# Gated delta rule with four operands to a norm, the first shift on TensorE, and modulation units placed by a weight

## The chip, the cores and the metric

One core of a Trainium2 chip. The metric is the device time of one execution of the whole program, in microseconds. All operands are fp32; the large projections are carried out as three matmuls each, on a weight and an activation that are split into a high and a low part.

## The reference

Two transformer blocks stand one behind the other, T = 256 tokens, D = 1024. Each norm is modulated by rows of `silu(c) @ w + b`, six rows of 1024 per layer in the first block, nine in the second. The first layer of the first block is attention, the second the gated delta rule:

```python
mod = (silu(c) @ ada_w[layer] + ada_b[layer])
shift_m, scale_m, gate_m, shift_f, scale_f, gate_f = split(mod, 6)
h = rmsnorm(x, norm_mix_g) * (1.0 + scale_m) + shift_m        # then attention or:
qkv = silu(conv(h @ w_in))                                    # 8 heads of 128
q = q * rsqrt(sum(q * q) + EPS) * 128 ** -0.5
k = k * rsqrt(sum(k * k) + EPS)
o = chunk_gated_delta_rule(q, k, v, g, beta)                  # decay, triangular inverse
o = rmsnorm(o, norm_g) * silu(z);  x = x + gate_m * (o @ w_out)
h = rmsnorm(x, norm_ffn_g) * (1.0 + scale_f) + shift_f;  x = x + gate_f * swiglu(h)
```

The second block has, in each of two layers, a half-step FFN, a mixing layer and another half-step FFN, on two streams of 256 tokens (the last FFN on one).

## The kernel before

Activations lie transposed, features on the partitions, in eight tiles of 128 x 256. A projection of one weight unit (1024 x 128) is 24 matmuls: eight tiles times three products (`mm3`, lines 405 to 407).

All weights come from memory in one list, `PLAN`, of 783 units of up to 512 KB. `mat` units feed matmuls. `mod` units are 128 columns of a modulation matrix, transposed; VectorE multiplies such a unit by the broadcast `silu(c)` and sums along the row (`mod_unit`, line 491), twice in the second block, whose two streams have a condition each. There are 240. `pump` (line 361) issues the loads on SP's queue up to twelve units ahead, into nine raw buffers, and splits up to three matmul units ahead: ScalarE casts (line 378), VectorE subtracts (line 379). `get` (line 384) hands out the next matmul unit and first works off the modulation units before it. `_evenly` (line 48) sets the modulation units at equal distances among a part's matmul units, after some at its front and before some at its end.

The instructions of each engine are put in one order when the program is built: by their place in the program and by when a planner thinks that their operands are there. Each engine then keeps to its order and waits where it must. A unit of modulation can so stand well ahead of the place that `PLAN` gives it.

The start (`build`, line 1412): the condition is loaded 128 times over, the positions too, the rope tables are made on VectorE, the squares of x are added up by GpSimd (line 551) and summed by a matmul with ones; eight `mod` units for the scale and eight for the shift go through VectorE, then `scale` (line 853), `shift` (lines 860, 861), and the first projection.

The delta-rule layer (`gdn`, line 1103): projections, convolutions and silu of heads 0 to 3; the norms (`gdn_norm`); decay and products of each head (`gdn_mats`); the inverse of two pairs of heads (`gdn_inverse`, line 1026), woven with the projections of heads 4 to 7; reading (`gdn_read`), and the same for heads 4 to 7, woven with the projections of z. A norm squares on ScalarE, sums over the partitions by a 128-column matmul of ones (line 559), which leaves the sum in all partitions, and runs `rsq` (line 515) for each operand of 256 columns: logarithm, exponential and a scaled copy on ScalarE, three instructions on VectorE (lines 522 to 524); then VectorE multiplies. There are 24 such operands: q and k of eight heads, and eight outputs.

The FFNs (`ffn`, line 623) run in three parts: gate and up units, then eight output units of the part. With two streams a matmul has 512 columns.

## Time and profile before

| what | value |
|---|---|
| runs, median of 3 | 2502.35 us (2498.07 to 2504.37) |
| profiled execution | 2497.55 us |
| its span, first to last instruction | 2495.7 us |
| mean granted TensorE clock | 0.994 |
| TensorE busy | 2391.3 us (96%) |
| VectorE busy | 1786.3 us (72%) |
| ScalarE busy | 1073.5 us (43%) |
| moved from memory | 408.66 MB, 164 GB/s over the span |

A page gives shares of the whole span; a stretch view gives the same for part of it. PE is TensorE, DVE VectorE, ACT ScalarE, POOL GpSimd, SP the engine that issues most loads. A busy TensorE has a matmul in flight, whose end is modelled; starts are measured.

### The profile page before, as it was taken

The page shows a single profiled execution, that of the slowest core. Times are in us where ns is not written, and L with a number is a line of the kernel's source. Part 1 is how long each engine was busy: PE and PEld are TensorE (multiplying, and loading weights), DVE is VectorE, ACT ScalarE, POOL GpSimd, SP SyncE. Part 2 cuts the span into 40 slices and gives each one's busy share as a digit, 9 for nine tenths or more (in the row PEclk, how much of TensorE's full clock was granted, in tenths as well). Part 3 has the DMA queues.
Part 4 walks back from the last instruction along what each step waited for, and adds up shares of the span by engine and source line. Part 5 has one row for each costly group of instructions (what it writes and reads, how often), then busy time and mean ns, then how long its engine had stood idle before and what let it go on. Part 6 is the DMA issues. An engine that isn't in the chain of part 4 may idle for free.

```text
span 2495.7 us, 38415 instructions
## 1 busy us (share of the span) xinstructions
PE 2391.3 (96%) x14963; PEld 2130.3 (85%) x14963; DVE 1786.3 (72%) x3087; ACT 1073.5 (43%) x1879; POOL 169.9 (7%) x172
## 2 busy tenths in 40 slices
PE   3999998899999999999999999999999999999998
PEld 2889998898999888888886888888988878988998
DVE  8987779886897997763657597663687663675765
ACT  3554455566644622223537432223432223456444
POOL 1000000414100100000010100000100000111000
PEclk9999999999999999999999999999999999999999
DMA  9766676432786475542220265452365452242652
GB/s 332 271 223 227 225 236 225 153 102 90 263 265 209 161 236 191 173 162 99 79 79 33 85 219 178 153 182 87 109 201 180 160 175 95 83 131 77 205 183 70
DMA packets 118406, 412.21 MB, mean 165 GB/s; under 512 B 13136, under 2 KB 16464, under 8 KB 118224
## 3 DMA queue, kind: packets, MB, share of 16 engines
q1 hardware_dynamic: 113904, 402.28, 47.7%
q10 hardware_dynamic: 4320, 7.47, 0.9%
q8 instruction: 118, 1.93, 0.3%
q14 instruction: 64, 0.52, 0.1%
HBM read 408.66 MB, written 1.05 MB: 164 GB/s over the span
## 4 chain that ended last, share of the span: by engine, by line
PE 76%; DVE 9%; DMA 8%; issue 3%; ACT 2%; POOL 1%; DVEq 0%; ACTq 0%; SPq 0%; POOLq 0%
PE pmm L405 21%; PE pmm L406 21%; PE pmm L407 21%; DMA r<-w 7%; DVE l L379 2%; DVE r L491 2%; DVE junk L491 2%; PE pax L1026 2%; PE pmm L1348 1%; PE pax L407 1%; PE pax L406 1%; PE pax L405 1%; PE pnm L1387 1%; PE pax L1358 1%; ACT h L378 1%
## 5 line engine op out<-in xcount | busy, mean ns | idle before, releaser
L378 ACT CAST h<-r 128x1024 fp32r<-128x1024 f32 (+2 forms) x543 | 549.6, 1017 | 992.4 <-PE pmm L406 907.3
L379 DVE TENSOR_TENSOR l<-r,h 128x1024 fp32r<-128x1024 f32 (+2 forms) x543 | 645.0, 1192 | 195.6 <-ACT h L378 188.2
L405 PE MATMUL pmm<-h,h 128*128 128x512 f32 (+1 forms) x1916 | 668.3, 350 | 31.3 <-ACT h L860 23.1
L406 PE MATMUL pmm<-h,h 128*128 128x512 f32 (+1 forms) x1916 | 664.7, 347 | 1.8 <-DVE h L593 1.6
L407 PE MATMUL pmm<-h,l 128*128 128x512 f32 (+1 forms) x1916 | 662.3, 346 | 0.0
L405 PEld LDWEIGHTS pmm<-h,h 128*128 128x128 f32 x1916 | 364.1, 190 | 78.1 <-ACT h L860 23.8
L406 PEld LDWEIGHTS pmm<-h,h 128*128 128x128 f32 x1916 | 364.2, 190 | 48.5 <-DVE h L593 3.7
L407 PEld LDWEIGHTS pmm<-h,l 128*128 128x128 f32 x1916 | 364.2, 190 | 44.7 <-issue 0.2
L405 PE MATMUL pmm<-hid,h 128*128 128x256 f32 (+1 forms) x1053 | 349.8, 332 | 6.2 <-DVE s L633 2.7
L406 PE MATMUL pmm<-hid,h 128*128 128x256 f32 (+1 forms) x1053 | 348.3, 331 | 1.5 <-DVE hid L444 1.5
L407 PE MATMUL pmm<-hid,l 128*128 128x256 f32 (+1 forms) x1053 | 348.0, 331 | 0.7 <-DVE l L379 0.7
L405 PE MATMUL pmm<-hb,h 128*128 128x258 f32 x1008 | 286.4, 284 | 5.7 <-ACT hb L581 4.2
L407 PE MATMUL pmm<-hb,l 128*128 128x258 f32 x1008 | 284.9, 283 | 0.0
L406 PE MATMUL pmm<-hb,h 128*128 128x258 f32 x1008 | 284.9, 283 | 0.0
L491 DVE SCALAR_TENSOR_TENSOR junk<-r,cnd 128x1024 f32<-128x1024 f32 x144 | 175.9, 1221 | 125.9 <-DMA r<-w 122.6
L405 PEld LDWEIGHTS pmm<-hid,h 128*128 128x128 f32 x1053 | 200.4, 190 | 26.3 <-ACT hid L443 3.9
L406 PEld LDWEIGHTS pmm<-hid,h 128*128 128x128 f32 x1053 | 200.4, 190 | 20.9 <-DVE hid L444 2.4
L407 PEld LDWEIGHTS pmm<-hid,l 128*128 128x128 f32 x1053 | 200.5, 190 | 19.3 <-DVE l L379 1.1
L405 PEld LDWEIGHTS pmm<-hb,h 128*128 128x128 f32 x1008 | 190.8, 189 | 7.3 <-ACT hb L581 5.0
L406 PEld LDWEIGHTS pmm<-hb,h 128*128 128x128 f32 x1008 | 191.7, 190 | 0.4 <-DVE hb L582 0.2
L407 PEld LDWEIGHTS pmm<-hb,l 128*128 128x128 f32 x1008 | 191.7, 190 | 0.1
L491 DVE SCALAR_TENSOR_TENSOR r<-r,cnd 128x1024 f32<-128x1024 f32 x144 | 176.1, 1223 | 5.5 <-ACT cnd L464 2.4
(332 smaller groups left out, 2867.8 us busy)
## 6 DMA issues: line engine op xcount, KB each, us to landing
r<-w SPq DMA_DIRECT2D x665, 512.0 KB, 4.2
r<-w SPq DMA_DIRECT2D x96, 448.0 KB, 3.4
r<-w SPq DMA_DIRECT2D x16, 256.0 KB, 2.5
cnd<-cond ACTq DMA_DIRECT2D x8, 512.0 KB, 4.6
r<-w SPq DMA_DIRECT2D x6, 384.0 KB, 3.2
const<-const SPq DMA_DIRECT2D x2, 960.0 KB, 6.3
x<-xT ACTq DMA_DIRECT2D x8, 128.0 KB, 5.7
x<-ctxT ACTq DMA_DIRECT2D x8, 128.0 KB, 2.6
```

Source lines behind the costliest of these rows:

```text
L378: nc.scalar.copy(h[:, :n], r[:, :n])
L379: nc.vector.tensor_tensor(lo[:, :n], r[:, :n], h[:, :n].bitcast(F32), op=OP.subtract)
L405: nc.tensor.matmul(out, wh, ah, start=start, stop=False)
L406: nc.tensor.matmul(out, wh, al, start=False, stop=False)
L407: nc.tensor.matmul(out, wl, ah, start=False, stop=stop)
L491: nc.vector.scalar_tensor_tensor(o, r, 1.0, self.conds[ns - 1 + s], op0=OP.mult, op1=OP.mult, accum_out=t[:, 8 * s + m:8 * s + m + 1])
L1026: nc.tensor.matmul(p[:, s], a[:, s], b[:, s], start=True, stop=True)
L1348: self.nc.tensor.matmul(s, q, k, start=True, stop=True)
L1358: self.nc.tensor.transpose(p[:, 128 * b:128 * b + 128], P[:, 128 * b:128 * b + 128], self.ident)
L1387: nc.tensor.matmul(o[64 * a:64 * a + 64, 128 * qt:128 * qt + 128], V[2 * s + b][:, h], pts[a][:, 128 * b:128 * b + 128], start=b == 0, sto ...
```

## The change

Four things change.

- The placement: `_place` spreads the modulation units by a weight (`room`) of each matmul unit instead of by count. In FFNs an output unit weighs 1.0, a gate or up unit 0.5, within a window. In the delta-rule layer the units stand behind those of heads 4 to 7 (weight 2) and of z (1); the eight of its scale move into the first FFN. `get` issues the loads and splits of all units passed before it works off their modulation.
- The start: the shift's eight units are taken untransposed as `rows` units; `mod_rows` multiplies them on TensorE by `silu(c)` in one of 32 columns, four quarters of 256 into four strips of 32 partitions, adds up over eight units, copies, transposes twice and adds the bias. The condition and positions are loaded as rows and spread by a matmul with ones; ones is set by GpSimd instead of loaded; the squares of x are added up by TensorE; half of the x loads go on SP's queue; the gain is finished column by column; the norm precedes the rope tables; the first query unit is taken ahead of the last two row units.
- The norms of the delta rule: four operands are summed into four strips of 32 partitions (`norms`), go through one `rsq`, and are spread again by a matmul with a selecting matrix (`spread`) into PSUM, from which VectorE multiplies 512 columns at once. The scale of q moves into `gdn_mats`.
- `rsq` has one `y` buffer instead of two.

```diff
-def _evenly(units, mods, a, b):
+def _place(units, mods, room):
+    room = [room(i, u[1]) for i, u in enumerate(units)]
+    out, k, c, total = [], 0, 0.0, sum(room)
+    for u, w in zip(units, room):
         out.append(u)
-        while k < len(mods) and i >= a + k * n // len(mods):
+        c += w
+        while k < len(mods) and c * len(mods) >= (k + 1 - 1e-6) * total:
             out.append(mods[k])
             k += 1
+    assert k == len(mods)
+def _ffn_room(a, b):
+    return lambda i, key: (1.0 if key[1] == "o" else 0.5) if a <= i < b else 0.0
...
-    u += _evenly(q, A(0, 2, 3, 4), 4, 0)
+    rows = [("rows", ("ada_w", 0, 0, kt), [("ada_w", 0, kt * 128, 0, 1024)]) for kt in range(KT)]
+    u = A(0, 1) + rows[:6] + q[:1] + rows[6:] + _place(q[1:], A(0, 2, 3, 4), lambda i, key: float(i >= 3))
-    u += _evenly(q[:16], A(0, 5), 2, 3) + _evenly(q[16:], A(1, 0, 1), 0, MODS_OUT)
+    u += _place(q[:16], A(0, 5), _ffn_room(2, 15)) + _place(q[16:], A(1, 0, 1, 2), _ffn_room(0, 46))
-    u += _evenly(q, A(1, 2, 3, 4, 5), 0, 4)
+    u += _place(q, A(1, 3, 4, 5), lambda i, key: 2.0 if key[0] in "qkv" and key[1] > 3 else float(key[0] == "z"))
+    u += _place(q[:16], B(0, 2), _ffn_room(5, 16)) + _place(q[16:], B(0, 3, 4, 5, 6, 7), _ffn_room(0, 46))
+    u += _place(q[:16], B(0, 8), _ffn_room(5, 16)) + _place(q[16:], B(1, 0, 1, 2, 3), _ffn_room(0, 46))
+    u += _place(_ffn_units(("f1", 1), "ffn1_w_in_2", "ffn1_w_out_2", 1), B(1, 4, 5, 6, 7, 8), _ffn_room(6, 60))
...
-    def pump(self):
+    def pump(self, look=LOOK):
+        nc = self.nc
+        while self.pd < min(len(PLAN), self.pos + look):
...
     def get(self, key):
-        self.flush()
+        if key in self.taken:
+            return self.taken.pop(key)
+        mods = self.passed(len(PLAN))
         i = self.pos
         assert PLAN[i][1] == key, (PLAN[i][1], key)
         self.pump()
         self.pos += 1
+        self.modulate(mods)
         return self.spl.pop(i)
+    def ahead(self, key):
+        u = self.get(key)
+        self.flush()
+        self.taken[key] = u
...
+    def spread_row(self, p, row):
+        self.nc.tensor.matmul(p, self.ones[0:1, :], row, start=True, stop=True)
...
+        if key[:3] == ("ada_w", 0, 1):
+            o, g = COLS["ada_b"][0] + KT + m, COLS["norm_mix_g"][0] + m
+            nc.vector.scalar_tensor_tensor(self.scale0[:, m:m + 1], t[:, m:m + 1], self.bias1[:, m:m + 1],
+                                           self.cols[:, g:g + 1], op0=OP.add, op1=OP.mult)
+        elif m == KT - 1:
...
+    def mod_rows(self, key, r):
+        nc = self.nc
+        kt = key[3]
+        if kt == 0:
+            self.pmod = self.ax()
+        p = self.pmod
+        for g in range(4):
+            nc.tensor.matmul(p[32 * g:32 * g + 32, :256], self.cond0[:, kt, :], r[:, 256 * g:256 * g + 256],
+                             start=kt == 0, stop=kt == KT - 1)
+        if kt < KT - 1:
+            return
+        e, q = self.t("u"), self.ax()
+        nc.scalar.copy(e, p[:, :256])
+        for h in range(2):
+            nc.tensor.transpose(q[:, 128 * h:128 * h + 128], e[:, 128 * h:128 * h + 128], self.ident)
+        v = q[:, :256].rearrange("p (h g q) -> p g h q", h=2, g=4)
+        t = self.mod[key[:3]] = self.keep(KT, "mod_first")
+        o = COLS["ada_b"][0]
+        nc.vector.tensor_tensor(t.rearrange("p (g h) -> p g h", h=2), v[:, :, :, 0],
+                                self.cols[:, o:o + KT].rearrange("p (g h) -> p g h", h=2), op=OP.add)
...
-        r, y, a = self.nrm("r", T, 3), self.nrm("y", T, 2), self.nrm("a", T, 2)
+        r, y, a = self.nrm("r", T, 3), self.nrm("y", T, 1), self.nrm("a", T, 2)
...
+        if st["tensor"]:
+            n = st["n"][0] = st["n"].get(0, 0) + 1
+            if n == 1:
+                st["p"][0] = self.psum("nm", 1)[:, :T]
+            nc.tensor.matmul(st["p"][0], self.ones, s[:, :T], start=n == 1, stop=n == tot)
+            return
...
-        nc.scalar.dma_start(pi, bass.AP(tensor=self.a["pos"].tensor, offset=self.a["pos"].offset,
-                                        ap=[[0, 128], [1, T]]))
+        nc.scalar.dma_start(pi[0:1, :], self.a["pos"])
         ang, kk, rr = self.t("u"), self.t("u"), self.t("u")
-        nc.vector.tensor_copy(kk, pi)
+        nc.vector.tensor_copy(kk[0:1, :], pi[0:1, :])
+        p = self.ax()[:, :T]
+        self.spread_row(p, kk[0:1, :])
         o = COLS["inv_freq"][0]
-        nc.vector.tensor_scalar(ang, kk, self.cols[:, o:o + 1], None, op0=OP.mult)
+        nc.vector.tensor_scalar(ang, p, self.cols[:, o:o + 1], None, op0=OP.mult)
...
+    def norms(self, rows, inv):
+        p = self.psum("nm", 1)[:, :T]
+        for g, v in enumerate(rows):
+            self.nc.tensor.matmul(p[32 * g:32 * g + 32], self.ones[:, :32], v, start=True, stop=True)
+        return self.rsq(p, inv)
+    def spread(self, r, gs):
+        p = self.ax()
+        for i, g in enumerate(gs):
+            self.nc.tensor.matmul(p[:, i * T:i * T + T], self.sel[:, g], r, start=True, stop=True)
+        return p
+    def squares(self, src):
+        s = self.nrm("sq", 512, 2)
+        self.nc.scalar.activation(s, src, AF.Square)
+        return [s[:, :T], s[:, T:]]
     def gdn_norm(self, qkv):
-        nc = self.nc
-        for qk, v in qkv:
-            st = self.stats(1)
-            self.push(st, qk, 0, 512)
-            rq, rk = self.rsq(st["p"][0], 1.0), self.rsq(st["p"][1], 1.0)
-            nc.vector.scalar_tensor_tensor(qk[:, :T], qk[:, :T], 128.0 ** -0.5, rq, op0=OP.mult, op1=OP.mult)
-            nc.vector.tensor_tensor(qk[:, T:], qk[:, T:], rk, op=OP.mult)
+        r = self.norms(sum([self.squares(qk) for qk, _ in qkv], []), 1.0)
+        for i, (qk, _) in enumerate(qkv):
+            self.nc.vector.tensor_tensor(qk, qk, self.spread(r, (2 * i, 2 * i + 1)), op=OP.mult)
...
-        for dst, rhs in ((lt, kb), (at, qk[:, :T])):
+            nc.vector.scalar_tensor_tensor(dst, g[:, :384], scale, dec, op0=OP.mult, op1=OP.mult)
...
-            os = self.t("os")
+            os.append(self.t("os"))
+            nc.scalar.copy(os[g], o)
+        r = self.norms(sum([self.squares(v) for v in os], []), 1.0 / 128)
+        w = COLS["gdn_norm_g"][0]
+        for g, v in enumerate(os):
+            nc.vector.scalar_tensor_tensor(v, v, self.cols[:, w:w + 1], self.spread(r, (2 * g, 2 * g + 1)),
+                                           op0=OP.mult, op1=OP.mult)
+            out += [v[:, :T], v[:, T:]]
...
+        self.sel = self.t("sel").rearrange("p (g c) -> p g c", g=4)
+        nc.gpsimd.memset(self.sel, 0.0)
+        for g in range(4):
+            nc.gpsimd.memset(self.sel[32 * g:32 * g + 1, g], 1.0)
...
-        self.gdn_norm(qkv[0])
+        for i in (0, 2):
+            self.gdn_norm(qkv[0][i:i + 2])
...
-        for t in qkv[1]:
-            self.gdn_norm([t])
+        for i in (0, 2):
+            self.gdn_norm(qkv[1][i:i + 2])
...
+        self.ones = self.keep(128, "ones")
+        nc.gpsimd.memset(self.ones, 1.0)
+        self.cond0 = self.t("og")[:, :32 * KT].rearrange("p (k c) -> p k c", k=KT)
+        nc.gpsimd.memset(self.cond0, 0.0)
...
+        rows = [self.t("og")[0:1, :] for _ in range(2)]
+        for i in range(2):
+            nc.scalar.dma_start(rows[i], a["cond"][0:1, 512 * i:512 * i + 512])
+        self.pump(2)
+        self.x = []
+        for k in range(KT):
+            t = self.xp.tile([128, 512], F32, name=f"x{k}")
+            (nc.sync if k % 2 else nc.scalar).dma_start(t[:, :T], a["xT"][:, k])
+            self.x.append(t)
+        self.pump()
+        self.conds = [right.tile([128, D], F32, name="cond"), None, None]
+        for i in range(2):
+            p = self.mm()
+            self.spread_row(p, rows[i])
+            self.act(self.conds[0][:, 512 * i:512 * i + 512], p, AF.Silu)
+        o = COLS["c"][0]
+        self.act(self.cond0[:, :, 0], self.cols[:, o:o + KT], AF.Silu)
+        self.scale0, self.bias1 = self.keep(KT, "scale0"), self.keep(KT, "bias1")
+        o = COLS["ada_b"][0] + KT
+        nc.vector.tensor_scalar(self.bias1, self.cols[:, o:o + KT], 1.0, None, op0=OP.add)
         self.table(LOG_SET)
-        st = self.stats()
+        st = self.stats(tensor=True)
         for k in range(KT):
...
+                r = self.rsq(st["p"][0], 1.0 / D)
+                self.rope = self.rope_tables()
                 self.flush(KT)
-                self.scale(st, self.gain("ada_w", 0, "norm_mix_g", 1))
+                self.c0 = self.load_consts(0, "cst0")
+                self.ident, self.triu = self.c0["ident"], self.c0["triu"]
+                self.scale(r, self.scale0)
                 self.flush()
+                self.ahead(("qa", 0))
```

## Rows read from the trace of the kernel before

**Rows 1.** The page, part 1: busy time and share of the span of each engine.
```profile
PE 2391.3 (96%) x14963; PEld 2130.3 (85%) x14963; DVE 1786.3 (72%) x3087; ACT 1073.5 (43%) x1879; POOL 169.9 (7%) x172
```

**Rows 2.** Waits of TensorE: waiter <- releaser: us in total, times, longest.
```profile
...
PE pmm L405 <- ACT h L860: 23.1, 1, 23.1
...
PE pax L987 <- DVE kb L984: 5.3, 2, 5.0
```

**Rows 3.** Six stretches, all engines (us, busy and instructions each, granted clock, DMA).
```profile
0.00:44.60 44.60, 2.07 (x4) 1.17 (x4) 33.01 (x70) 13.57 (x22) 4.97 (x9) 1.00 0.95 352
49.30:85.00 35.70, 35.70 (x239) 32.82 (x239) 34.36 (x54) 15.99 (x24) 8.25 (x8) 1.00 0.90 317
183.00:380.00 197.00, 193.30 (x1587) 191.77 (x1586) 150.95 (x239) 95.44 (x173) 6.21 (x5) 0.99 0.69 230
379.60:389.00 9.40, 2.73 (x10) 1.43 (x8) 9.26 (x18) 3.98 (x8) 0.00 (x0) 0.72 0.93 333
443.00:475.00 32.00, 23.51 (x153) 21.48 (x153) 28.48 (x64) 17.23 (x40) 11.22 (x11) 0.89 0.26 86
475.00:531.00 56.00, 55.28 (x471) 54.28 (x470) 42.50 (x74) 30.36 (x53) 23.67 (x22) 1.00 0.47 156
```

**Rows 4.** Two stretches, VectorE's instructions of line 491 alone.
```profile
379.60:389.00 9.40, 3.67 (x6) 0.72 0.93 333
...
475.00:531.00 56.00, 14.79 (x23) 1.00 0.47 156
```

**Rows 5.** Groups by line and shape, 0 to 45 us: count, busy us, mean ns.
```profile
L491 DVE SCALAR_TENSOR_TENSOR r<-r,cond 128x1024 f32<-128x1024 f32 x16 | 19.4, 1216 | 8.0 <-DMA r<-w 8.0
L379 DVE TENSOR_TENSOR l<-r,h 128x1024 fp32r<-128x1024 f32 x4 | 4.8, 1216 | 0.0
...
L491 DVE DVE_READ_ACCUMULATOR r<-r,cond 128x1 f32 x16 | 1.3, 80 | 0.0
```

**Rows 6.** Timeline of ScalarE at the start: begin, length, what.
```profile
29.47 1.28 ACT L451 ACT_TABLE_LOAD   x1
...
30.77 0.47 ACT L464 ACTIVATE y<-pnm,eps1e-06_155 128x256 f32<-128x256 f32 x1
...
33.12 1.04 ACT L378 CAST h<-r 128x1024 fp32r<-128x1024 f32 x1 [0.98 <-DMA r<-w]
```

**Rows 7.** DMA, 0 to 45 us in 40 bins: GB/s.
```profile
GB/s 0 93 184 342 261 143 402 426 408 382 385 399 362 379 144 379 422 422 426 411 408 411 411 408 411 415 408 411 408 411 411 408 411 408 411 408 226 324 255 309
```

**Rows 8.** Chain that ended last: begin, length of one piece.
```profile
495.88 1.79 PE pax L1026 x16
```

**Rows 9.** Timeline of TensorE: 64-column strips (128*64), then a full one.
```profile
1328.56 1.09 PE L1387 MATMUL pnm<-pt,h 128*64 128x128 f32 x16
1329.58 0.70 PE L1348 MATMUL pmm<-h,raw 128*128 128x512 f32 x1
```

**Rows 10.** Timeline of TensorE, first projection.
```profile
44.64 1.01 PE L405 MATMUL pmm<-h,h 128*128 128x256 f32 x3 [23.09 <-ACT h L860]
...
49.74 0.28 PE L405 MATMUL pmm<-h,h 128*128 128x256 f32 x1
```

**Rows 11.** Groups by line and shape, VectorE, 394 to 638 us.
```profile
L1050 DVE TENSOR_TENSOR dt<-dt,pax 128x512 f32<-128x512 f32 x24 | 16.4, 683 | 18.9 <-PE pax L1026 18.8
...
L522 DVE TENSOR_TENSOR a<-y 128x256 f32<-128x256 f32 x24 | 9.4, 428 | 3.8 <-ACT y L464 3.4
```

**Rows 12.** Timeline of VectorE, a two-stream FFN, output units.
```profile
1904.90 1.23 DVE L491 SCALAR_TENSOR_TENSOR junk<-r,cnd 128x1024 f32<-128x1024 f32 x1 [1.31 <-DMA r<-w]
...
1910.61 1.23 DVE L491 SCALAR_TENSOR_TENSOR junk<-r,cnd 128x1024 f32<-128x1024 f32 x1 [1.29 <-DMA r<-w]
```

**Rows 13.** Timeline of ScalarE there.
```profile
1904.55 1.06 ACT L378 CAST h<-r 128x1024 fp32r<-128x1024 f32 x1 [4.34 <-PE pmm L406]
1909.99 1.06 ACT L378 CAST h<-r 128x1024 fp32r<-128x1024 f32 x1 [4.38 <-PE pmm L406]
```

More of the change, by code (lines that the diff above doesn't have):

```diff
@@ L215, in constants @@
     c["ident"] = np.eye(128)
-    c["ones"] = np.ones((128, 128))
     c["triu"] = (p[:, None] <= p[None, :]) * 1.0
@@ L273 @@
 CONST = constants()
-CONST_GROUPS = (("ident", "ones", "triu", "half", "rot1"),
+CONST_GROUPS = (("ident", "triu", "half", "rot1"),
                 ("tril", "trimid", "upper", "m_causal", "m_sb", "m_lev"),
@@ L318, in __init__ @@
         self.raw, self.spl = {}, {}
-        self.mod = {}
+        self.mod, self.taken = {}, {}
         self.nt = 0
@@ L389, in get, with passed, modulate @@
         self.pos += 1
+        self.modulate(mods)
         return self.spl.pop(i)
-    def flush(self, n=len(PLAN)):
-        end = self.pos + n
-        while self.pos < min(end, len(PLAN)) and PLAN[self.pos][0] != "mat":
-            self.pump()
-            r = self.raw.pop(self.pos)
-            self.mod_unit(PLAN[self.pos][1], r)
-            self.pos += 1
+    def ahead(self, key):
+        u = self.get(key)
+        self.flush()
+        self.taken[key] = u
+    def passed(self, n):
+        out, end = [], min(len(PLAN), self.pos + n)
+        while self.pos < end and PLAN[self.pos][0] != "mat":
+            self.pump()
+            out.append((PLAN[self.pos], self.raw.pop(self.pos)))
+            self.pos += 1
+        return out
+    def modulate(self, mods):
+        for (kind, key, _), r in mods:
+            (self.mod_unit if kind == "mod" else self.mod_rows)(key, r)
+    def flush(self, n=len(PLAN)):
+        self.modulate(self.passed(n))
     def mm3(self, out, u, j, ah, al, start, stop, w=128):
@@ L984, in gdn_mats @@
         nc.vector.tensor_tensor(kb, qk[:, T:], b[:, :T], op=OP.mult)
-        for dst, rhs in ((lt, kb), (at, qk[:, :T])):
+        for dst, rhs, scale in ((lt, kb, 1.0), (at, qk[:, :T], 128.0 ** -0.5)):
             g = self.ax()
@@ L1060, in gdn_read @@
         G = range(len(mats) // 2)
-        uv, out = {}, []
+        uv, os, out = {}, [], []
         for g in G:
```

46 lines of the change are left out of this document (8 added, 38 removed), and 2 rows, old and new, of the table PHASES.

## The prediction

> **What bounds the kernel now.** I read the page first. TensorE has work in flight in 2391.3 of 2495.7 us [rows 1], so at most some 104 us can be won by filling gaps, and everything that adds matmul time to a full stretch costs its full length. Then the waits of TensorE alone [rows 2]: one wait of 23.1 us for the first shifted operand at the start, and 5.3 us, 5.0 of it in one piece, for the k-beta operand of the delta rule. Third, the stretches that hold these waits [rows 3]. In the first 44.6 us TensorE works 2.07 us, VectorE 33.0 and the DMA engines are 95% busy. From 379.6 to 389.0 (end of the first FFN, entry of the delta-rule layer) TensorE works 2.7 of 9.4 us. From 443 to 475 (norms and matrices of heads 0 to 3) 23.5 of 32.0, at a mean granted clock of 0.89. From 475 to 531 (inversion beside projections) 55.3 of 56: full. Part of VectorE's work is the modulation, a long multiply-reduce and a short read of the accumulator per unit: 6 such instructions in the entry, 23 in the inversion [rows 4], and 16 units before the first projection, 1.22 us each, 19.4 in all, with 16 reads of 0.08 [rows 5].
>
> The sum is made against the profiled execution: span 2495.7, time 2497.55, 1.85 us around it. That is 4.8 us under the median of the three runs (2502.35); I form the difference from the trace and take it off the median. A run can tell about 0.3%, 7.5 us.
>
> **The start.** At present the order is: 16 modulation units on VectorE, scale, shift, first matmul at 44.64. VectorE is the bound: 33.0 us of work from about 8 us on. The change takes the shift's 8 units off VectorE (half of 19.4: 9.7 us), the splits of the second to fourth weight unit need not be over either (3 x 1.22 [rows 5]), and eight column updates of the gain come in. The trace has none of these; the one-column read is 0.08 us, the 1024-wide multiply 1.22 [rows 5], so eight cost 0.6 to 9.8 us; I take 0.1 each, near the read, as they have one column. That leaves 33.0 - 9.7 - 3.7 + 0.8 = 20.4 us, from about 7 us on: 27.5 us. So the bound becomes the DMA. The cast of the first weight unit, the 17th unit in order, starts at 33.12 as soon as it lands [rows 6]. In the new order the 17th is the last row unit. Ahead of it the broadcast condition (512 KB), the broadcast positions (128 KB) and 64 KB of ones disappear: 0.72 MB at the 411 GB/s of the steady bins is 1.75 us, and the six slow first bins (93 to 143 GB/s where those transfers stand) may give 1.4 us more [rows 7]. The last row unit lands between 30.0 and 31.4 us; I take 30.5.
>
> Behind it stands a new chain: four row matmuls, a copy, two transposes, an add, the first shift. A 256-column fp32 matmul is two instructions of 256 columns, as long as four of 128; 16 of those take 1.79 us [rows 8], so it is 0.45 us, twice that at the low clock. The four go to four 32-column strips of the array. The trace shows strips of 64 columns only: 16 passes there take 1.02 us, start to next start, instead of 1.79 [rows 9], so strips overlap. Bounds for a row unit: 0.45 (all overlap, fast clock) to 3.6 (none, slow clock); I take 0.9. With copy 0.42, transposes 0.5, add 0.2, shift 0.45 and half a microsecond of hand-overs the first projection matmul starts at 33.5 instead of 44.64: 11.1 us. The squares of x move from GpSimd adds to eight fp32 matmuls of 0.9 us at the low clock; they lie before 20 us, where TensorE is idle. The x loads that move to SP's queue stand behind two units only. The constants' load now stands behind nine, and its first user is the transposes. A row matmul waits on TensorE for its landing; behind it are queued the other row units and the first projection, which needs them anyway.
>
> Two corrections. Now 28 units have been loaded by 44.6, eleven more than the first matmul needs; afterwards two. The projections take 2.9 us each and the DMA brings a unit in 1.28, so they aren't starved, but VectorE, already 34.4 of 35.7 us busy from 49.3 to 85 [rows 3], has three splits (3.6 us) still before it. I charge 2 us (between 0 and 3.6). From 44.64 a projection's matmul takes 0.41 us, at 49.74 it takes 0.28 [rows 10]: 4.7 us at the lower of the two clock levels (1.2 and 2.4 GHz). Row matmuls beforehand may have raised it; worth 0 to 2.3 us, I take 1. Start: -10, between -5 and -13.
>
> The norm now precedes the rope tables, so the activation tables change twice more. A load takes 1.28 us and the next activation follows it without a gap, 29.47 to 30.77 [rows 6]; ScalarE is 13.6 of 44.6 us busy, so I cost it at nothing, 1.3 if a load stands before the shift. The Trainium skill ("ScalarE: Activation LUTs", What ACT_TABLE_LOAD costs) gives a switch about 2.66 us including a drain; the row shows no drain behind the load, and by the page the uncovered price would be 2.7 instead of 1.3.
>
> **Placement of the units.** All 240 modulation units stay; only their places move. Eight leave the delta-rule layer for the first FFN, whose VectorE is busy 151 of 197 us [rows 3]; hidden, and 9.8 us if it were not. Forty units now begin right behind the layer's first weights and are pulled forward: six instructions, three units of 1.22 us, stand between the norm's chain in the entry [rows 4]. Afterwards no unit comes before head 4's query, so they go: 3.7 us off a wait in which VectorE is 9.3 of 9.4 us busy. I take -2.5, since splits will fill in part (0 to -3.7). Head 4 to 7 get 24 units where the inversion stands; twelve run there now. Twelve more are 15.6 us on a VectorE that is 42.5 of 56 us busy [rows 3], but six or so find room before, where the norms shrink. Nothing, between -1 and +4. In the FFNs I take 0 (-6 to +5): the first one idles 3.7 us of 197 on TensorE [rows 3], and such stalls will move more than go.
>
> **The norms of the delta rule.** Now each of 24 operands has its chain: three VectorE instructions of 0.43 and a multiply of the same width [rows 11]. After: six chains (18 x 0.43 = 7.7 us) and twelve 512-wide multiplies with a PSUM operand, 0.683 each by the same form in the inversion [rows 11], 8.2 us. 72 x 0.43 + 24 x 0.43 = 41.3 becomes 15.9 on VectorE; ScalarE loses 54 of 72 activations of that width. What of it counts is the stretch 443 to 475: 8.5 us idle. For four heads VectorE falls from 4 x 8 x 0.43 = 13.8 to 6 x 0.43 + 4 x 0.683 = 5.3 us. I leave 3 us of idling (two chains still run one behind the other): -5.5. The clock below full there costs 3.4 us of its stretch (32 x 0.11); half goes: -1.5.
>
> Against it stands TensorE. The spreading adds 24 matmuls of 0.45 = 10.8 us. The sums' 24 x 0.45 become six groups in four strips, 2.7 us, between that and 10.8 without overlap: net +2.7, +10.8 at worst. The layer is full in the inversion and afterwards, so I let all of it count. The strips cost a change of mode: the 16 strip passes take 1.02 us where eight pairs would take 0.90 [rows 8, 9], 0.12 more; as much again on the way in makes 0.25 per group, 1.5 for six (0 to 3). The Trainium skill ("TensorEngine Tiling (Array Packing)", Key Properties) says that a change of tiling mode drains TensorE; the row agrees, with 0.12 us. Were that only the last strip's tail and the rule without weight here, the sum would be 1.5 us lower. The scale of q moves into a multiply that exists already: nothing. With one y buffer a second chain's logarithm waits for the first chain's square; at the five two-stream entries that is up to 0.9 us each (two activations of 0.47 [rows 6]), beside the first stream's projections: nothing, 4.5 if uncovered. The second reading saves perhaps 0.5 us of its chain. Norms: -5.5 - 1.5 + 2.7 + 1.5 - 0.5 = -3.3.
>
> **Sum.** -10 - 2.5 + 0 - 3.3 = -15.8, say -16: 2481.5 in a profiled execution, 2486 against the median.
>
> **The rivals.** *VectorE stays the bound of the start.* Its instructions stand in a fixed order, and each early wait for a late transfer holds everything behind it; it already waits 8 us for the first unit. The rope tables now come after the norm. If they and the splits fall between the last scale and the shift, the first matmul comes at 39: 5.5 us less, -10.5, 2492. Against it: 20 us of work in 26.
>
> *The norms pay nothing.* The chain of two heads needs both, and spreading waits behind projections on TensorE; no idle time goes (+7), and strips don't overlap (+8 at worst, half of it taken): -16 + 7 + 4 = -5, 2497, no measurable change. For it: TensorE is full on both sides of the stretch.
>
> *The clock and the stalls give more.* The clock at the start gives 2.3 instead of 1, 1 us instead of 3 stays of the 8.5, the rest of that stretch's clock loss (1.9) and 6 us of the FFNs' stalls go too: -16 - 1.3 - 2 - 1.9 - 6 = -27, 2475. For it: these waits all stand behind VectorE, which gets lighter; against it: what is late next then is a load.
>
> *Slower: the modulation outruns VectorE in the output parts of the two-stream FFNs.* There a unit now follows the last after 5.7 us, each as its load lands [rows 12], while ScalarE casts a weight unit for TensorE every 5.44 [rows 13]. With weight 1.0 on output units and 0.5 on the others, an output part of eight units gets eight to ten modulation units instead of seven or eight: 10 x 5.7 = 57 us against 43.5, 13.5 behind. What covers it is the look-ahead of nine buffers, some four weight units or 22 us, and the lighter hidden parts after it. It decides once the cover is under 13.5 us; at 5 to 6 us uncovered in each of six parts it is +33, so +17 in all: 2519. Against it: VectorE idles a quarter of the time there.
>
> **How the numbers follow.** Forecast 0.55, late VectorE 0.17, norms pay nothing 0.09, more 0.11, slower 0.08. The forecast's own range, from its unknown costs, is 2478 to 2494. Faster by over 0.3% (under 2494.8): 0.53 of the forecast, 0.13 of late VectorE and 0.11, 0.77; slower (over 2510): 0.08; the rest 0.15. The range 2473 to 2499 leaves out the slow case and the ends.
>
> **What would show it.** First projection matmul at 33.5 (39 in the first rival); four strip matmuls of one row unit starting within 0.1 us; no modulation between the sums and the shift at the layer's entry; the wait for k-beta under 3 us; idle time of 443 to 475 down by 5; three VectorE instructions of the norm's kind 18 times instead of 72. It is wrong if TensorE's waits behind VectorE in the output parts grow, or if the start gains under 5 us.

## The result and the profile after

The changed kernel takes 2471.56 us (median of 4 runs, 2467.25 to 2473.51), the kernel before 2501.05 (4 runs, 2498.07 to 2504.37): 29.5 us less, ratio 0.9879, 95% interval 0.9861 to 0.9898. The forecast was 2486: right in direction, 14 us short, and 1.4 us outside its range. The two profiled executions, 2497.55 and 2473.51 us, lie 24.0 us apart where the forecast had 16: the one before is faster than its kernel's four runs, the one after the slowest of its four.

Page of the changed kernel, part 1 (answers to [rows 1]): 20.5 us more of TensorE work in flight, in a span 24 us shorter.
```profile
PE 2411.8 (98%) x15095; PEld 2139.4 (87%) x15095; DVE 1755.1 (71%) x3011; ACT 1058.2 (43%) x1830; POOL 173.1 (7%) x174
```

Waits of TensorE after (answers to [rows 2]): the 23.1 us for the first shift are gone, smaller waits for transfers stand there now. The wait for k-beta (line 1064, before 5.3 us) is down to 0.3.
```profile
PE pax L543 <- DMA r<-w: 6.5, 8, 2.6
PE pmm L501 <- DMA og<-cond: 4.5, 1, 4.5
PE pmm L428 <- ACT h L652: 4.3, 2, 3.5
PE pax L550 <- DMA const<-const: 2.8, 1, 2.8
...
PE pax L1064 <- DVE kb L1061: 0.3, 1, 0.3
```

Five stretches of the changed kernel (columns as in [rows 3]): start up to the first projection matmul, attention's first projections, entry of the delta-rule layer, norms and matrices of heads 0 to 3, inversion. The fourth row answers to the fifth of [rows 3]: TensorE idled 8.5 us there and now 1.3, and the granted clock rose from 0.89 to 1.00.
```profile
0.00:35.50 35.50, 18.35 (x88) 6.76 (x88) 22.68 (x59) 15.85 (x26) 0.67 (x6) 0.85 0.96 360
40.20:76.00 35.80, 35.80 (x237) 33.22 (x237) 33.38 (x52) 15.50 (x24) 9.22 (x8) 0.98 0.93 351
...
370.60:379.00 8.40, 4.24 (x20) 3.23 (x19) 6.58 (x14) 4.36 (x9) 1.31 (x5) 0.84 0.54 180
432.00:463.00 31.00, 29.69 (x218) 27.57 (x216) 26.87 (x52) 14.32 (x29) 16.66 (x14) 1.00 0.33 108
463.00:519.00 56.00, 54.39 (x455) 51.87 (x453) 49.17 (x84) 32.12 (x56) 24.45 (x19) 1.00 0.66 220
```

The modulation's instructions alone (line 518 now, multiplies and short reads) in the entry and the inversion, against 6 and 23 in [rows 4]:
```profile
370.60:379.00 8.40, 0.00 (x0) 0.84 0.54 180
463.00:519.00 56.00, 21.93 (x32) 1.00 0.66 220
```

Where the 24.0 us lie I read from the casts of the 543 weight units, which come in the same order in every kernel: how much earlier (minus) or later than in the kernel before each stage was passed, in us. The table has all traces of this study, and the sections below draw on it.
```
                    start,  first   entry  rest of  second  first   mixer,   second   rest  sum
                    attent. FFN            layer    FFN     two-s.  2nd two- two-s.
                                                            FFN 1   s. FFN 1 FFN 1
changed kernel      -8.9   -0.3    -1.5    -8.3    +1.5    -1.8    +1.6     -6.1     0.0  -23.9
norms alone         +0.1   +0.2     0.0    -7.0    -0.2    +0.8    +1.4      0.0     0.0   -4.7
places and order    +1.2   -3.2    -4.2    -0.5    -0.3    +2.9    +4.8     -6.1    +0.3   -5.1
start alone         -8.9   +0.5    -0.1    +1.7    +0.5    +0.4    +3.9     +1.3     0.0   -0.9
changed, full sums -12.3   +1.2    -3.4    -4.9    +1.3    +5.4    +1.1     -6.1     0.0  -17.6
order alone         -0.6   -0.3    -0.2    +1.1    +0.8    +3.1    +1.4     +3.4     0.0   +8.7
places alone        +1.9   -1.7    -3.1    +0.6    +0.4     0.0    +0.7     -6.1    +0.3   -7.0
no landing wait     +2.0   -2.4    -3.8    -5.9    +1.7    +1.5    -1.4     -6.1     0.0  -14.4
changed, const.     -7.9   +1.5    -4.1    -8.8    +1.9    -1.8    +2.1     -6.1     0.0  -23.3
changed, no l.wait  +3.6   -4.0    -2.9   -11.3    +3.6    -0.2    -1.2     -6.1     0.0  -18.6
places in the layer -0.2   -0.7    -3.5    +0.5    -1.1    +2.6    +1.9     +2.9     0.0   +2.4
places in the FFNs  +2.5   -1.8    +3.2    +1.0    +0.5     0.0    +3.0     -6.1     0.0   +2.3
64 bytes            -0.6   -0.4    -0.2    -0.6    -0.7    +0.1    +3.4     +2.0     0.0   +3.1
changed, warm       -9.0   +1.9    -3.1    -8.8     0.0    -1.8    +4.3     -6.1     0.0  -22.7
changed, one old   -12.1   +0.1    -3.0    -8.7    +0.2    -1.8    +1.2     +3.3     0.0  -20.6
```
Single stages differ by a few us between executions of kernels that do the same there. The last FFN column does not: all seven traces with the new places and both without the wait are 6.1 us ahead (the stage takes 339.6 us), while the seven with the old places take 345.7 to 349.1.

### The profile page after: what moved, and what is told of

Same layout as the page of the kernel before. It is cut to its first block, busy times and chain, and to the rows that moved or that the text cites. A ratio compares the mean times of both kernels' runs of the same rounds, so it can differ in the third digit from the quotient of the medians.

```text
span 2471.7 us, 38558 instructions
## 1 busy us (share of the span) xinstructions
PE 2411.8 (98%) x15095; PEld 2139.4 (87%) x15095; DVE 1755.1 (71%) x3011; ACT 1058.2 (43%) x1830; POOL 173.1 (7%) x174
## 4 chain that ended last, share of the span: by engine, by line
PE 81%; DVE 7%; DMA 6%; issue 4%; ACT 1%; POOL 1%; DVEq 0%; ACTq 0%; POOLq 0%; SPq 0%
PE pmm L429 22%; PE pmm L428 22%; PE pmm L430 22%; DMA r<-w 5%; DVE l L385 2%; DVE r L518 1%; PE pax L1103 1%; PE pmm L1428 1%; PE pax L430 1%; PE pax L429 1%; PE pax L428 1%; PE pnm L1467 1%; PE pax L1438 1%; DVE junk L518 1%; ACT h L384 0%
## 5 line engine op out<-in xcount | busy, mean ns | idle before, releaser
L659 DVE SCALAR_TENSOR_TENSOR x<-pmm,mod_w_mod,x 128x256 f32<-128x256 f32 x188 | 84.6, 480 | 148.8 <-PE pmm L430 148.5
```

Source lines behind the costliest of these rows:

```text
L659: self.nc.vector.scalar_tensor_tensor(v, p[:, s * T - c0:s * T + T - c0], gate[:, 8 * s + m:8 * s + m + 1], v, op0=OP.mult, op1=OP.add)
```

## The parts one by one

*The norms alone*, in the kernel before:
```diff
+        r = self.norms(sum([self.squares(qk) for qk, _ in qkv], []), 1.0)
+        for i, (qk, _) in enumerate(qkv):
+            self.nc.vector.tensor_tensor(qk, qk, self.spread(r, (2 * i, 2 * i + 1)), op=OP.mult)
```


> The kernel before with the new norms of the delta rule alone (one chain for two heads, sums in four strips, spreading by TensorE; old start, old places of the units). My prediction's term for this part: -3.3 us. The two traces read together say about -7 us for the delta-rule layer behind its entry (the changed kernel is 11 us ahead where the gates begin and 18 us ahead at the layer's end). Theory A, the norms alone do it: -7 us, and the idle time of TensorE in the stretch of the first norms and matrices falls from 8.5 to under 2 us. Theory B, part of it belongs to the modulation units that were taken out of that stretch: only -3 to -4 us, and 3 us or more of idle time stay there.

Ratio 0.9968 (0.9957 to 0.9978): 8.0 us less, 5.5 to 10.8. Theory A holds. The stretch of the first norms, to be set beside the fifth row of [rows 3], without any change of the places:
```profile
440.00:469.00 29.00, 28.39 (x215) 26.44 (x213) 25.41 (x52) 13.34 (x26) 8.70 (x9) 1.00 0.41 129
```
0.6 us of idle time is left, and the clock is at its full level.

*Places and order*, and each by itself. The places are the calls of `_place` for `_evenly`; the order is this:
```diff
-        self.flush()
+        mods = self.passed(len(PLAN))
         ...
         self.pos += 1
+        self.modulate(mods)
```


> The kernel before with the new places of the modulation units alone, and with the new order inside a fetch (the splits of the next weight unit ahead of the modulation on VectorE); old start, old norms. My prediction: -2.5 us, all at the entry of the delta-rule layer, nothing in the FFNs. The traces read together: about -2 us at the entry and about -6 us in the FFNs, 5 of them around one stall near 2001 us, so -8 us. Theory B of the run above puts another -3 us here. If the stall near 2001 us is a chance of one execution, it is -3 us.

> The kernel before with the new order inside a fetch alone: the splits of the next weight unit stand ahead of the modulation units on VectorE, whose places in the list of units are the old ones. Places and order together took 14 us off the median (interval 9 to 19), where the prediction had 2.5. Theory A, the order does it (a split that TensorE is about to need no longer waits behind a modulation unit that waits for its landing): -9 to -12 us. Theory B, the places do it (fewer units where VectorE is full, none before the entry's shift): -2 to -4 us. The prediction had nothing for the order.

> The kernel before with the new places of the units alone, old order inside a fetch. Theory A: -2 to -5 us, most of it at the entry of the delta-rule layer. Theory B: -10 to -12 us. The prediction: -2.5 us.

Places and order: 0.9944 (0.9925 to 0.9963), 14.0 us less, 9 to 19. Order alone: 1.0006 (0.9996 to 1.0016), nothing. Places alone: 0.9950 (0.9931 to 0.9968), 12.5 us less, 8 to 17. Theory B: the places do it, five times what I had given them. Their two halves:
```diff
# in the layer and ahead of it
-    u += _evenly(q, A(1, 2, 3, 4, 5), 0, 4)
+    u += _place(q, A(1, 3, 4, 5), lambda i, key: 2.0 if key[0] in "qkv" and key[1] > 3 else float(key[0] == "z"))
# in the FFNs (one of six lines)
-    u += _evenly(_ffn_units(("f1", 1), ...), B(1, 4, 5, 6, 7, 8), MODS_IN, MODS_OUT)
+    u += _place(_ffn_units(("f1", 1), ...), B(1, 4, 5, 6, 7, 8), _ffn_room(6, 60))
```


> The kernel before with new places in and ahead of the delta-rule layer alone (eight units moved from there to the first FFN; none between head 0's and head 4's first weights). The prediction's terms: -2.5 at the entry and nothing in the inversion. If the 12.5 us of the new places come from the entry and the layer: -8 us or more. If they come from the FFNs: -2 to -4 us.

> The kernel before with new places in the FFNs alone (weights 1.0 and 0.5 by part; the delta-rule layer as it was). The prediction: 0, between -6 and +5. By the other ends of the run above: -8 to -10 us if the 12.5 us come from the FFNs, -1 to -4 us if from the layer and its entry. The second rival on the other side, units that outrun VectorE in the output parts: slower than before.

In the layer: 0.9978 (0.9964 to 0.9992), 5.5 us less, 2 to 9; in the table the entry is the one stage clearly ahead (-3.5). In the FFNs: 0.9979 (0.9968 to 0.9989), 5.3 us less, 2.8 to 8; in the table the one steady gain is the 6.1 us of a single FFN. Neither expectation of the shares was right: they are halves. The slower rival has no support: over the three two-stream FFNs TensorE waits 2.8 to 5.1 us for hidden operands in the seven traces with the new places and 5.7 to 10.5 in those with the old; only in the second of these FFNs is it not less (1.3 to 3.6 against 0.8 to 2.6).

*The start alone.*
```diff
+            nc.tensor.matmul(p[32 * g:32 * g + 32, :256], self.cond0[:, kt, :], r[:, 256 * g:256 * g + 256],
+                             start=kt == 0, stop=kt == KT - 1)
```


> The kernel before with the new start alone (shift by TensorE rows, broadcast on the chip, order of the first loads and of the rope tables). My prediction: -10 us, the first projection matmul at 33.5 instead of 44.64. The traces: the changed kernel's first projection matmul comes at 35.5, and it is about 8.5 us ahead after the first attention. So -8.5 us by the traces, -10 by the prediction; under -5 would mean that the gain leans on the new places of the units behind it.

0.9959 (0.9944 to 0.9975): 10.3 us less, 6 to 14. The three parts by themselves add up to 8.0 + 14.0 + 10.3 = 32.3, the whole is 30.3 by its ratio: within the intervals they add.

## One stall in one FFN

VectorE of the kernel before where the stall near 2001 us falls (begin, length, what, and in brackets the wait before it):
```profile
1999.78 1.23 DVE L491 SCALAR_TENSOR_TENSOR junk<-r,cnd 128x1024 f32<-128x1024 f32 x1 [2.00 <-DMA r<-w]
...
2002.20 0.68 DVE L643 TENSOR_TENSOR s<-s,pmm 128x512 f32<-128x512 f32 x1
...
2003.80 0.69 DVE L444 TENSOR_TENSOR hid<-s,hid 128x512 fp32r<-128x512 f32 x1
```
A modulation unit waits 2 us for its load; behind it, in VectorE's fixed order, stands the hidden operand (lines 643 and 444) of the next output matmuls. The last matmul that this operand comes from started at 1996.83, so it could have been worked on soon after; it is begun at 2002.20, behind the unit's second multiply. Waits of that stretch, 1985 to 2010 us: ScalarE's cast of the hidden operand waits 4.9 us for line 643, TensorE 2.3 for the cast.
```profile
ACT hid L443 <- DVE s L643: 7.7, 2, 4.9
...
PE pmm L405 <- ACT hid L443: 2.3, 1, 2.3
```
In the ten us around it TensorE starts 24 matmuls, where it started 45 in the ten before; it idles 2.75 us, and the granted clock is 0.83:
```profile
1990.00:2000.00 10.00, 10.00 (x45) 8.26 (x44) 5.56 (x12) 2.87 (x4) 0.00 (x0) 1.00 0.63 200
2000.00:2010.00 10.00, 7.25 (x24) 5.31 (x23) 8.70 (x14) 1.55 (x2) 0.00 (x0) 0.83 0.51 169
```
Over the stage TensorE idles 3.4 us longer than in the changed kernel, and the clock costs 1.7 (10 x 0.17): 5.1 of the 6.1 us. All seven traces with the old places wait at the same two places of this FFN, the last hidden operand of the first and of the second part (0.6 to 2.4 us and 1.1 to 4.5), and none of the nine others waits there.

In the changed kernel VectorE waits even longer in front of the same operand, 4 us, but the load comes at 1975.72, while TensorE still works on the matmuls that the operand comes from (the last begins at 1977.85). The unit is over at 1978.14 and in nobody's way:
```profile
1975.72 1.23 DVE L518 SCALAR_TENSOR_TENSOR junk<-r,cnd 128x1024 f32<-128x1024 f32 x1 [4.00 <-DMA r<-w]
...
1978.14 1.08 DVE L385 TENSOR_TENSOR l<-r,h 128x896 fp32r<-128x896 f32 x1
1979.14 0.68 DVE L703 TENSOR_TENSOR s<-s,pmm 128x512 f32<-128x512 f32 x1
```
So the changed kernel with the old places in this FFN alone:
```diff
-    u += _place(_ffn_units(("f1", 1), ...), B(1, 4, 5, 6, 7, 8), _ffn_room(6, 60))
+    u += _evenly(_ffn_units(("f1", 1), ...), B(1, 4, 5, 6, 7, 8), 10, 10)
```


> The changed kernel with the old, even places of the forty modulation units in one FFN alone, the last but one (first two-stream FFN of the second layer). If the places there are what counts: TensorE's idle time in that stage goes from 0.5 back to 4 us or more, and the kernel is 4 to 6 us slower than the changed kernel (ratio to before 0.990 where that has 0.988). If the lighter norms and the earlier start had taken the stall away: 0.5 us idle stays, and no difference. The prediction had 0 for this term.

Ratio 0.9898 (0.9883 to 0.9913) against 0.9879: by the medians some 5 us slower, though the intervals overlap. The trace is plain: the stall is back. Waits of TensorE in this FFN, one operand and one place in the order (lines moved by 12 against the changed kernel):
```profile
PE pmm L440 <- ACT hid L478: 5.1, 2, 4.2
```
The stage takes 349.0 instead of 339.6 us. The first branch of the expectation holds; neither the lighter norms nor the earlier start would have taken the stall away.

*The wait itself*, in the kernel before and in the changed one:
```diff
+            if key[:2] != ("ada_w", 0) or ch > 1:
+                o = r = self.conds[ns - 1 + s]
```


> The kernel before; every modulation unit but the first sixteen multiplies the condition tile that is there already instead of the unit that was loaded (all loads stay, and so does the time of each VectorE instruction; the modulation's values are not the reference's). VectorE no longer waits for the landing of such a unit. Theory C, places and order gain because VectorE, whose order is fixed, waited for late landings with TensorE's operands behind it: -12 us or more against before, as much as places and order, and less spread between runs. Rival D, what they gain is VectorE's own work at full places (the instructions, not the wait): -4 us or less, since all the work is still there.

> The changed kernel without the wait for the landing of modulation units (as in the run of the kernel before without that wait: all but the first sixteen multiply a tile that is there already; loads and VectorE time stay, the modulation's values are not the reference's). That took 21 us from the kernel before, the new places 12 to 14. Theory E, the new places leave a part of the waits: the changed kernel goes down by another 5 to 9 us (ratio to before 0.984 to 0.986). Rival F, what is left of TensorE's idle time behind the start (28 us in the trace) has other causes: less than 2 us (0.987 to 0.988).

Before: 0.9914 (0.9899 to 0.9929), 21.5 us less. Theory C, with a reservation: with the dependence gone the program also orders VectorE's work otherwise. In the table 5.9 us of its gain lie in the rest of the delta-rule layer, where the new places alone give nothing and the norms are the old ones; how much of the wait in the norms is the chain and how much landings or order, the runs don't separate. In the second run the new order is dear; from 31.87 us on seven multiplies, with three splits among them, stand ahead of the shift's last step, which comes at 43.91 instead of 34.75:
```profile
31.87 1.22 DVE L521 SCALAR_TENSOR_TENSOR cond<-cond 128x1024 f32<-128x1024 f32 x1
...
43.91 0.16 DVE L558 TENSOR_TENSOR mod_first<-pax,cols 128x8 f32<-128x8 f32 x1
```
Its ratio, 0.9895 (0.9880 to 0.9911), is neither theory E's nor rival F's: the start comes 12.5 us later (table), of which 7.2 are made up afterwards. So neither run prices the wait cleanly. What both show: in the FFN of the stall nothing is left to win over the new places (339.6 in all), while in the first FFN 2 to 4 us may be.

## The start

From the changed kernel's timeline of TensorE: the last row unit, the transposes, the first projection matmul.
```profile
30.16 1.08 PE L543 MATMUL pax<-r,og 128*32 128x256 f32 x8 [0.19 <-DMA r<-w]
34.05 0.66 PE L550 MATMUL pax<-const,u 128*128 128x128 f32 x2 [2.81 <-DMA const<-const]
35.51 1.01 PE L428 MATMUL pmm<-h,h 128*128 128x256 f32 x3 [0.80 <-ACT h L920]
...
41.78 0.28 PE L430 MATMUL pmm<-h,l 128*128 128x256 f32 x1
```
The row unit is there at 30.16 (forecast 30.5); then 2.8 us go by for the constants. So an earlier load:
```diff
         self.pump(2)
+        self.c0 = self.load_consts(0, "cst0")
```


> The changed kernel with the constants' load right behind the first two weight units instead of behind nine. At its start TensorE waits 2.8 us for the constants, of which the transposes need the identity. Theory: first projection matmul at 33 instead of 35.5, and 2 to 3 us less than the changed kernel in all (ratio to before 0.9870 where that has 0.9879). Rival: the load delays the row units by its own 0.8 us and the clock, which is at half there, keeps the rest: no change of the total that can be measured.

0.9883 (0.9865 to 0.9901): no difference from the changed kernel. The wait for the constants is gone, but the row units come later by as much, and the first projection matmul starts at 36.15:
```profile
31.79 1.08 PE L543 MATMUL pax<-r,og 128*32 128x256 f32 x8 [3.62 <-DMA r<-w]
33.09 1.08 PE L543 MATMUL pax<-r,og 128*32 128x256 f32 x8 [0.21 <-DMA r<-w]
34.66 0.69 PE L550 MATMUL pax<-const,u 128*128 128x128 f32 x2 [0.49 <-ACT u L548]
```
The transfers bound the start (DMA share 0.96 up to 35.5), whichever of them the wait names. The other price is the clock:
```diff
+        for _ in range(4 if kt == KT - 1 else 1):
+            nc.tensor.matmul(self.pwarm[:, :T], self.ones, self.x[kt][:, :T], start=True, stop=True)
```


> The changed kernel with eleven more 256-column matmuls of x in the gaps of TensorE at the start, one behind each of the first seven row units and four behind the last, into a PSUM tile that nobody reads. In the changed kernel the granted clock is 0.5 from 28.1 to 41.8 us, and the first 6.3 us of projections run at half rate. Theory: with the gaps filled the clock stays at or comes back to full before the projections begin, which is worth up to 3.1 us (half of 6.3). Rival: the clock is back earlier, but the splits and loads behind it (VectorE is 5.0 of 5.0 us busy from 35 to 40, the DMA engines at 1.03) take the gain back: under 1 us at the end of the attention. A second rival: the clock stays low and the matmuls delay the transposes: 1 to 2 us slower.

0.9877 (0.9856 to 0.9897), again no difference. Stretches of this run:
```profile
30.00:35.00 5.00, 3.66 (x32) 1.83 (x32) 3.04 (x6) 3.12 (x5) 0.00 (x0) 1.00 0.99 374
35.00:40.00 5.00, 3.43 (x14) 2.96 (x15) 4.92 (x8) 4.58 (x10) 0.00 (x0) 0.68 1.02 411
40.00:45.00 5.00, 5.00 (x42) 5.00 (x41) 4.73 (x9) 3.01 (x6) 0.00 (x0) 0.98 1.03 410
```
The clock is full before the projections and falls in the stretch in which TensorE waits 1.79 us for the constants; the first projection matmul comes at 36.98, 1.5 us later than in the changed kernel. The lower level ends 1.6 us earlier, so 3.2 us of the projections run at it instead of 6.3, worth 1.5 us, and at the end of the attention nothing is left (-9.0 against -8.9). That is the first rival's outcome; what takes the gain back is the later first matmul.

## Sums over the whole array, and an address

```diff
-            self.nc.tensor.matmul(p[32 * g:32 * g + 32], self.ones[:, :32], v, start=True, stop=True)
+            self.nc.tensor.matmul(p, self.blk[:, 96 - 32 * g:224 - 32 * g], v, start=g == 0, stop=g == len(rows) - 1)
```


> The changed kernel, with the sums of the delta rule's norms as four matmuls over the whole array, one behind the other into one accumulation, instead of four 32-column strips side by side. The prediction counts 0.45 us for a strip group and 0.25 us for its two changes of mode against 1.8 us for four full matmuls: six groups of 1.1 us, +6.6 us against the changed kernel, as everything in that layer counts. Rival: the groups stand where TensorE waits for the chain anyway, so +1 us or less for four of the six groups, and under +3 us in all.

0.9890 (0.9871 to 0.9908) against 0.9879: 2.8 us by the ratios, whose intervals are some 9 us wide. In the table the entry and the layer together are 1.5 us behind the changed kernel and 3.4 to 4.6 behind the three other traces that have the same layer (constants, warm, one old): less than my 6.6, and on both sides of the rival's 3. Timeline of TensorE in the changed kernel around a group of four sums and a spreading, and then where a later group begins (x2 is one 256-column matmul):
```profile
430.77 0.28 PE L430 MATMUL pmm<-h,l 128*128 128x256 f32 x1
430.98 0.64 PE L1014 MATMUL pnm<-sq,ones 128*32 128x256 f32 x8
431.55 0.38 PE L428 MATMUL pmm<-h,h 128*128 128x256 f32 x1
...
432.01 1.89 PE L1021 MATMUL pax<-r,sel 128*128 128x256 f32 x8
...
518.72 0.62 PE L1014 MATMUL pnm<-sq,ones 128*32 128x256 f32 x2
519.27 1.99 PE L1021 MATMUL pax<-r,sel 128*128 128x256 f32 x8
```
Four sums take 0.57 us from start to next start, and the step into them is 0.21 instead of 0.12: 0.66 against the 0.45 + 0.25 counted. The four strips of a group begin within 0.02 us of each other, as foretold; eight passes of spreading start 0.216 us apart. But only two of the six groups stand like that. The order of the program splits the other four into two visits each (two and two sums, or one and three), and a visit takes 0.55 to 0.57 us, whether it holds one sum (518.72 to 519.27) or four. The ten visits take 5.6 us; the full sums take 9.4 in the run that has them. So the strips save TensorE 3.8 us and not 6.6, and the 3.4 to 4.6 us fit that. That groups stand where TensorE waits anyway is not shown. The Trainium skill ("TensorEngine Tiling (Array Packing)", Key Properties) has a change of tiling mode drain TensorE; the trace agrees, with 0.09 us on the way in.

This run loses elsewhere: 7.2 us against the changed kernel in the first two-stream FFN, without a wait. All matmuls there have 512 columns and TensorE is full; yet in the same 270 us it gets through fewer of them. Stretch of TensorE alone in the kernel before, the changed one and the one with full sums:
```profile
880.00:1150.00 270.00, 270.00 (x1184) 1.00 0.53 179
```
```profile
880.00:1150.00 270.00, 270.00 (x1193) 1.00 0.53 169
```
```profile
880.00:1150.00 270.00, 270.00 (x1169) 1.00 0.54 168
```
From start to next start, a gate or up matmul takes 228.9, 226.7 and 233.1 ns on average, an output matmul 226.7 to 226.8 in all three; 960 gate and up matmuls at 6.4 ns make 6.1 of the 7.2 us. What differs: the weight tiles begin at byte 84,128 of each partition, at 84,192 and at 85,088, since the kernels keep other small tiles below them; the moving operand of the gate and up matmuls lies at the same addresses in all. So:
```diff
+        self.keep(16, "pad")
```


> The kernel before with one unused tile of 64 bytes per partition among the constants, so that every weight tile lies 64 bytes higher, where it lies in the changed kernel. In the first two-stream FFN the same 512-column matmuls of the gate and up parts take 228.3 ns on average in the kernel before (229 to 232 many of them), 226.7 in the changed kernel, 231 in the variant with sums over the whole array, each with the weights at another address and the moving operand at the same one. Theory: the address of the weight against the moving tile sets it, so 226.7 here and about -2 us in that stage. Rival: it is something else in the new start, and 228.3 stays.

The total doesn't show it: 1.0004 (0.9992 to 1.0015). The stretch does, with 0.16 us of idle time in it:
```profile
880.00:1150.00 270.00, 269.84 (x1191) 1.00 0.56 179
```
226.7 ns per gate or up matmul, as in the changed kernel: 64 bytes are worth (228.9 - 226.7) ns x 960 = 2.1 us here. The stage's +0.1 in the table hides it: in this trace, as in seven others, the clock falls to its lower level at the FFN's start, for 3.4 us or more, and each 3.4 us cost 1.7. The four traces with the weights at 84,192 and without that fall have -1.8, the three with both -0.2 to +0.4. All sixteen traces go by the address: eight at 84,128 with 228.9 ns, seven at 84,192 with 226.7, one at 85,088.

## Why the prediction was right and where it was wrong

- **Start, forecast -10: right in size, not in its make-up, and so by luck.** Alone -10.3; in the trace -8.9 (to -12.3 in other traces of the same start), and 1.8 more in the first two-stream FFN, by the address that the new start moved. The DMA bound the start as forecast and the row unit landed on time; I had named the constants' first user but not charged the wait, so the first projection matmul came at 35.5 and not 33.5. The clock term had the wrong sign: row matmuls did not raise it, and the lower level lasts 6.3 us of the projections (35.5 to 41.8) instead of 4.7. (The 4.7 are read from steps of 0.213 us against 0.117; the granted clock of that stretch is shown as 1.00.) The two misses are 2.0 us and 1.8 (0.8 lost where 1 was taken as gained), and the 2 us charged for VectorE's splits did not come: the first matmul is 9.1 us earlier, and 8.9 are left at the end of the attention.
- **Entry, forecast -2.5: right.** -1.5 in the changed kernel, -2.9 to -4.2 in the eight other traces with the layer's new places; no modulation stands there any more.
- **Inversion, forecast 0: right.** The three runs with the layer's new places and the old norms have -0.5 to +0.6 in the rest of the layer, and in the changed kernel 32 instructions of the modulation instead of 23 stand in the inversion, where TensorE is busy 54.4 of 56 us (before 55.3).
- **Norms, forecast -3.3: mis-sized, -7 to -8.** The step that failed is "I leave 3 us of idling" and "half goes" for the clock. Idle time in the stretch fell by 7.9 and not 5.5 (to 0.6 in the run with the norms alone), in the whole rest of the layer from 14.1 to 5.0 us (first two rows below: before and norms alone), and the clock gave back 3.4 and not 1.5: its lower level, 6.8 us long before, doesn't come in this layer any more. TensorE's net was mis-sized too, the other way: spreading 10.5 us, the sums 5.6 instead of 9.9, +6.2 against +4.2, since six groups came as ten visits. -9.1 - 3.4 + 6.2 = -6.3, against -7.0 in the table. The chain runs 6 times as forecast (three instructions each; last row, one of the three in the changed kernel).
```profile
420.40:629.70 209.30, 195.16 (x1522) 186.51 (x1522) 163.82 (x328) 127.18 (x264) 67.73 (x74) 0.98 0.40 127
420.70:623.20 202.50, 197.50 (x1572) 186.08 (x1572) 143.90 (x262) 110.52 (x210) 64.47 (x73) 1.00 0.43 132
415.00:610.00 195.00, 2.55 (x6) 1.00 0.41 134
```
- **FFNs, forecast 0: wrong, and the largest miss.** The failed step: "such stalls will move more than go". I judged them from the first FFN, 3.7 us of 197, and didn't follow the one at 2001 us to its cause. It comes at a fixed place, where in the trace read above a modulation unit with a late load stands in front of a hidden operand that is due. The stage is longer in all seven traces with the old places and in none with the new, by 6.1 us in the profiled execution of before.
- **From the trace to the median: a further miss.** I took the difference from one execution of the kernel before, which lies 3.5 us under the median of its kernel's runs; that of the changed kernel lies 2.0 above its own. These are the 5.5 us between 24.0 and 29.5. In the FFN of the stall the execution of before has, with one other, the shortest time of the seven with old places (345.7; mean 347.5), in the mixer and the FFN ahead of it the shortest of all that wait for landings. On average the new places give 8 us there and not 6; that is part of it. The rest is spread over stages and not settled.
- **The rivals.** What came is the rival that gives more (2475): the FFN's stall, nearly all idle time of the norms, the whole of their clock loss; only its better clock at the start didn't come. VectorE did not stay the bound of the start. The norms paid. The slower case did not show.

## What to carry to other kernels

A stall behind an engine with a fixed order is found by asking what stands behind the waiting instruction and when that is due, not how long it waits: in one FFN 4 us of waiting cost nothing with the new places, and 2 us cost some 4.8 with the old (21 matmuls of 0.227 us fewer in ten us). A small stall that falls at the same place of the program in several traces is a term of its own and not noise; one execution may show it at its smallest. Where transfers bound a stretch, moving the one that the wait names only gives the wait another name.

## What the hardware showed that I had not expected

- The same full-rate matmuls take 226.7, 228.9 or 233.1 ns from start to start, depending on the address of the weight tiles while the moving operand stays where it is; 64 bytes decide between the first two. Why, no run here tells.
- A visit to 32-column strips between matmuls over the whole array took 0.55 to 0.57 us, with one 256-column sum in it or with four side by side; one such matmul over the whole array takes 0.43. Packing paid with two sums or more in a visit, not with one.
- A wait in the norms cost its own length and 3.4 us of clock behind it; the clock was at its lower level for 6.8 us there before, and not at all after.
- The clock fell while a row unit came every 1.3 us. The granted clock was 0.50 from 21.3 to 24.7 us, 1.00 to 28.1 and 0.50 to 41.8; a row unit takes 0.64 us at the upper level and 1.08 at the lower. Before the first fall TensorE had waited 2.6 us and then worked 0.7 of 1.3; the second came within a wait of 1.9.
